# Attention by pairs of heads: 64-row score products side by side and a stacked position product

## The chip, the cores and the metric

The kernel runs on one core of a Trainium2 chip. The metric is the time of one execution on the device, in microseconds (us); the median of three runs before is 3395.38 us (3394.99 to 3407.65).

## What is computed

Two layers of a hybrid backbone over 1024 latent and 256 context tokens. Each layer mixes tokens by three parallel groups (latent attention with 8 heads, a convolution, a long convolution "hyena") and then runs an expert mixture. The change is in the attention:

```python
s = (jnp.einsum('bqhd,bkhd->bhqk', qn, k_nope, ...)      # 64 position-free dims
     + jnp.einsum('bqhr,bkr->bhqk', qr, k_rope, ...))    # 32 rotated dims, one key for all heads
w = jax.nn.softmax(s * scale, axis=-1).astype(v.dtype)
return jnp.einsum('bhqk,bkhd->bqhd', w, v)
```

Latent queries read 1280 keys (latent and context), context queries the 256 context keys (layer 0 only).

## The kernel before

Products that need more than one pass of precision are split: an operand `x` is kept as `xh` and `xl` (`hilo`, ScalarE rounds, VectorE subtracts), and `mm3` (lines 93 to 97) makes three products, high by high, high by low, low by high, into one bank of PSUM.

In `mla` the heads are taken one by one. For each head `K0`/`K1` (128 x 1280) holds 64 rows of position-free keys, the 32 rows of the rotated key, copied in by `fixed`, a row of ones and zeros; `Q0`/`Q1` (128 x 1024) holds the query the same way, with minus the greatest score of each query in row 96. So one product over 128 rows gives the score less its maximum. The maxima come from `largest`: a 96-row product of high parts for each 128 queries and up to 512 keys into a bank `p`, a VectorE reduction `mx`, and at the end a transposition `p<-ident,m` that puts the maxima into row 96.

`attend` runs units: a unit is one key tile of 128 keys and two lanes of 512 queries. For each lane `score` makes three products into a bank `s` (two banks), and ScalarE's exponential writes `pt`. `pv` makes the value product `o`: the two lanes go to columns 0 to 63 and 64 to 127 of the array. GpSimd adds up the `pt` for the denominators (`psum`). In a window of ten units (one head) the steps of `prepare` for the next head (`queries`, `keys`, `largest`) are dealt out over slots between the units. Before a window's last unit the rest of the steps is emitted at once. The convolution and `hyena` are emitted behind the first window and the scheduler moves them into gaps; what stands where on an engine is settled at build time, each engine then runs its list in order. `heads` loads the weights of the next head on SyncE's queue.

PSUM has eight banks: `s=2, o=1, p=3, hx=1, ha=1` (`hx` and `ha` are for the convolution and hyena).

Of the kernel before, what the change touches and what calls it, by code (L numbers as in the profile page):

```python
# [51 lines left out]
class Kernel:  # L52
# [17 lines left out]
    def banks(self, es, **tags):  # L70

        assert sum(tags.values()) <= 8
        self.n += 1
        pool = es.enter_context(self.tc.tile_pool(name=f"psum{self.n}", bufs=1, space=bass.MemoryType.PSUM, reuse_waits="tile"))

        def ps(tag, shape=(128, 512)):
            self.n += 1
            return pool.tile(list(shape), F32, name=f"{tag}{self.n}", tag=tag, bufs=tags[tag])
        return ps
# [317 lines left out]
    def win(self, l, M):  # L397
# [3 lines left out]
        with ExitStack() as es:  # L401
# [3 lines left out]
            with ExitStack() as es2:  # L405
# [24 lines left out]
                for g0, g1 in ((0, 4), (4, 8), (8, 10)):  # L430
# [65 lines left out]
                    S.activation(M["kr"][64:96, sl], tq[3][0:32, :N], AF.Copy)  # L496
                    V.tensor_tensor(M["kr"][96:128, sl], tq[3][0:32, :N], M["kr"][64:96, sl].bitcast(F32), ALU.subtract)
            with ExitStack() as es2:
# [3 lines left out]
                self.heads(l, 0, M)  # L502
                sc = self.t(P, [128, 6, 4], F32, "scols", bufs=1)
# [91 lines left out]
    def mla(self, l, M):  # L595
# [3 lines left out]
        with ExitStack() as es:  # L599
            P = self.pool(es, f"mla{l}", 2, **({} if last else {"side": "right"}))  # L600
            H = self.pool(es, f"hy{l}", 1)
            ps = self.banks(es, s=2, o=1, p=3, hx=1, ha=1)
# [4 lines left out]
            Qs, Ks, Cs = [], [], []  # L607
            for i in range(2):
                Qs.append(operand(f"Q{i}", 1024))
                Ks.append(operand(f"K{i}", 1280))  # L610
                Cs.append(None if last else operand(f"QC{i}", 256))

            def fixed(i):

                K = Ks[i]
                S.activation(K[0][64:96, :], M["kr"][64:96, :].bitcast(F32), AF.Copy)
                S.activation(K[1][64:96, :], M["kr"][96:128, :].bitcast(F32), AF.Copy)
                G.memset(K[0][96:128, :].bitcast(F32), 1.0)
                G.memset(K[1][96:128, :].bitcast(F32), 0.0)
                for Q in (Qs[i], Cs[i]):  # L620
                    for x in Q or ():
                        G.memset(x[96:128, :].bitcast(F32), 0.0)

            Vt = [None] * 10
            self.turned = {}

            def values(i):

                wr = self.t(P, [128, 512], F32, "rd", bufs=1)[:, :256]
                wh, wl = (self.t(M["pool"], [128, 2, 128], F32R, f"wq{x}", bufs=1).rearrange("p a b -> p (a b)") for x in "hl")  # L630
                nc.sync.dma_start(wr, A["w_v"][l][:, 256 * i:256 * i + 256])
                self.hilo(wh, wl, wr)
                for k in range(10):
                    p = ps("p")[:, :256]
# [6 lines left out]
            def prepare(h):  # L641

                K, Q, QC = Ks[h % 2], Qs[h % 2], Cs[h % 2]
                if h == 0:
                    fixed(0)
                elif h == 1:
                    with self.tc.issue_after(self.turned[0].ins):
                        fixed(1)
                yield from self.queries(P, ps, l, h, M, Q, QC, tab)
                yield from self.keys(P, ps, l, h, M, K)  # L650
                yield from self.largest(P, ps, K, Q, 1024, 0, 1280, h == 0)
                if QC:
                    yield from self.largest(P, ps, K, QC, 256, 1024, 256, h == 0)

            windows = []
            for h in range(8):
                w = []
                if h % 2 and not last:
                    w += self.attend(P, ps, l, [(h - 1 + j, Ks[j], Cs[j], 0, 256, 1024) for j in range(2)], Vt, range(8, 10))
                w += self.attend(P, ps, l, [(h, Ks[h % 2], Qs[h % 2], c, 512, c) for c in (0, 512)], Vt, range(10))  # L660
                windows.append(w)
            units = [u for w in windows for u in w]
            vals = values(0)
            for i, _ in enumerate(prepare(0)):
                if i >= 6:
                    next(vals, None)
            for _ in vals:
                pass
            units[0].score(0)
            units[0].score(1)  # L670
            n, later = 0, []
            for h, w in enumerate(windows):

                chain, steps = (prepare(h + 1), 33 if last else 38) if h < 7 else (iter(()), 0)
                vals, valued = values(1) if h == 3 else None, 0
                taken, slots = 0, 3 * len(w) - SLACK[l]
# [6 lines left out]
                for i, u in enumerate(w):  # L683
                    if n + 1 < len(units):
# [3 lines left out]
                        units[n + 1].score(0)  # L688
                        slot(3 * i)
                        units[n + 1].score(1)  # L690
                    slot(3 * i + 1)
# [6 lines left out]
                    slot(3 * i + 2)  # L698
# [10 lines left out]
    def queries(self, P, ps, l, h, M, Q, QC, tab):  # L709

        nc, A, S, V, G = self.nc, self.A, self.S, self.V, self.G
        wr = M["wq"]
        wh = self.t(M["pool"], [128, 2, 128], F32R, "wqh", bufs=1)
        wl = self.t(M["pool"], [128, 2, 128], F32R, "wql", bufs=1)
        self.hilo(wh, wl, wr)
        kr, kh, kl = M["wk"], self.t(M["pool"], [128, 64], F32R, "wkh", bufs=1), self.t(M["pool"], [128, 64], F32R, "wkl", bufs=1)
        self.hilo(kh, kl, kr)
        M["wkhl"] = kh, kl
        if h < 7:
            with self.tc.issue_after(self.loaded.ins):  # L720
                self.heads(l, h + 1, M)
        for c, N in ((0, 512), (512, 512), (1024, 256))[: 3 if QC else 2]:
            p = ps("p")
            s = slice(c, c + N)
# [23 lines left out]
    def largest(self, P, ps, K, Q, nq, k0, nk, first):  # L748

        V = self.V  # L750
# [84 lines left out]
    def hyena(self, l, M, P, ps):  # L835
# [12 lines left out]
        def table(src):  # L848

            t = self.t(P, [128, 2, 512], F32R, "ht", bufs=6)[:, :, :src.shape[2] * src.shape[3]].rearrange("p h (k m) -> p h k m", k=src.shape[2])  # L850
            with self.tc.issue_after(self.turned[0].ins):
                G.dma_start(t, src)
# [947 lines left out]
```

## Time and profile before

| | |
|---|---|
| median of three runs | 3395.38 us |
| the profiled execution | 3398.4 us, its span 3396.6 us |
| PE (TensorE), DVE (VectorE), ACT (ScalarE), POOL (GpSimd) busy | 3126.6, 2532.4, 1691.3, 1300.8 us |
| attention stage of layer 0 | about 500 to 975 us |
| attention stage of layer 1 | about 2200 to 2625 us |

Matmuls are pipelined on PE, and an instruction's duration holds a tail that lies beside the next one; what a product costs in a stream is the distance from its start to the next start. The name behind an arrow is written from the names after it, so `s<-Q1h,K1h` is a score with moving queries and stationary keys. `128*64` is rows by columns of the array in use.

### The profile page before, as it was taken

How to read it: one execution, taken by the hardware profiler on the slowest of the kernel's cores; microseconds unless marked ns; L12 is line 12 of the kernel's file. 1: busy time of each engine (PE TensorE's matmuls, PEld its weight loads, DVE VectorE, ACT ScalarE, POOL GpSimd, SP SyncE). 2: the span in 40 equal slices, each digit the busy share in tenths (PEclk: the TensorE clock that was granted, in tenths of full speed). 3: DMA queues.
4: the chain of work that ended last, by engine and by line, in shares of the span. 5: the costliest groups of instructions: out<-in, count | busy, mean ns of one | idle time of the engine just before them, and what ended most of it. 6: DMA issues, size and time to landing. Idle time of an engine off the chain costs nothing. (4 is left out here: it accounts for less than half of the span.)

```text
span 3396.6 us, 42699 instructions
## 1 busy us (share of the span) xinstructions
PE 3126.6 (92%) x15595; PEld 2226.8 (66%) x15595; DVE 2532.4 (75%) x3507; ACT 1691.3 (50%) x2447; POOL 1300.8 (38%) x1130
## 2 busy tenths in 40 slices
PE   7898989999999699999999969899999959999996
PEld 2467865666567466666666657656664747888885
DVE  7755698777667677777777646977775769998986
ACT  4315235433443356555665543353435427777775
POOL 4431255754654312211211112565557423433334
PEclk9898989999999799999999979899999979999998
DMA  8981112231253477777777621221223459999994
GB/s 304 324 272 60 38 64 82 54 101 45 73 162 116 179 288 280 275 298 279 289 280 284 217 95 44 82 70 51 69 93 115 151 225 356 385 378 372 380 379 173
DMA packets 138075, 660.80 MB, mean 195 GB/s; under 512 B 20520, under 2 KB 58824, under 8 KB 107145
## 3 DMA queue, kind: packets, MB, share of 16 engines
q1 hardware_dynamic: 112681, 582.85, 45.7%
q0 software_dynamic: 24768, 74.05, 7.9%
q8 instruction: 123, 2.02, 0.2%
q10 hardware_dynamic: 416, 1.18, 0.1%
q14 instruction: 87, 0.71, 0.1%
HBM read 589.24 MB, written 68.78 MB: 194 GB/s over the span
## 5 line engine op out<-in xcount | busy, mean ns | idle before, releaser
L91 DVE TENSOR_TENSOR mwl<-raw,mwh 128x1024 fp32r<-128x1024 f32 x710 | 883.4, 1281 | 215.8 <-ACT mwh L90 203.6
L90 ACT ACTIVATE mwh<-raw 128x1024 fp32r<-128x1024 f32 x768 | 791.0, 1057 | 347.9 <-PE acc L97 112.3
L96 PE MATMUL acc<-mwl,xh 128*128 128x512 f32 x1024 | 404.3, 395 | 0.5 <-DVE idc L1371 0.5
L97 PE MATMUL acc<-mwh,xl 128*128 128x512 f32 x1024 | 401.7, 394 | 0.1
L95 PE MATMUL acc<-mwh,xh 128*128 128x512 f32 x1024 | 371.4, 400 | 6.3 <-ACT xh L90 5.9
L803 POOL TENSOR_TENSOR psum<-psum,pt 128x512 f32<-128x512 f32 x252 | 333.1, 1341 | 68.3 <-ACT pt L788 64.4
L788 ACT ACTIVATE pt<-s 128x512 f32<-128x512 f32 (+1 forms) x336 | 196.0, 587 | 251.9 <-PE s L97 209.7
L1500 POOL DMA_INDIRECT xd<-ymoe,idx x31 | 105.5, 3404 | 544.5 <-DVE ymoe L1496 468.0
L758 DVE TENSOR_REDUCE mx<-p 128x1 f32<-128x512 f32 (+1 forms) x374 | 204.2, 584 | 65.0 <-PE p L100 64.2
L95 PEld LDWEIGHTS acc<-mwh,xh 128*128 128x128 f32 x1024 | 191.4, 189 | 69.0 <-ACT mwh L90 11.3
L96 PEld LDWEIGHTS acc<-mwl,xh 128*128 128x128 f32 x1024 | 192.9, 188 | 43.8 <-DVE mwl L91 2.5
L91 POOL TENSOR_TENSOR mwl<-raw,mwh 128x1024 fp32r<-128x1024 f32 x58 | 150.0, 2591 | 183.2 <-ACT mwh L90 121.1
L97 PEld LDWEIGHTS acc<-mwh,xl 128*128 128x128 f32 x1024 | 191.8, 188 | 39.5 <-issue 0.8
L100 PE MATMUL o<-pt,Vt 128*64 128x512 f32 (+1 forms) x672 | 184.1, 611 | 0.0
L564 DVE SCALAR_TENSOR_TENSOR cacc<-pad,cw,cacc 128x1295 f32<-128x1295 f32 (+1 forms) x90 | 165.7, 1842 | 1.3
L97 PE MATMUL mm<-hTh,wfl 128*128 128x512 f32 (+1 forms) x400 | 151.4, 380 | 12.8 <-DVE wfl L91 12.8
L95 PE MATMUL mm<-hTh,wfh 128*128 128x512 f32 (+1 forms) x400 | 152.7, 382 | 4.0 <-ACT wfh L90 4.0
L96 PE MATMUL mm<-hTl,wfh 128*128 128x512 f32 (+1 forms) x400 | 152.1, 380 | 0.0
L562 POOL TENSOR_TENSOR cacc<-cacc,tap 128x1295 f32<-128x1295 f32 (+1 forms) x30 | 97.0, 3233 | 120.8 <-ACT tap L561 118.7
L100 PE MATMUL cx<-raw,xcT 128*32 128x512 f32 x1024 | 124.0, 597 | 0.0
L95 PE MATMUL mm<-woh,yhh 128*128 128x512 f32 x280 | 114.8, 413 | 6.7 <-ACT wt L1128 3.8
L96 PE MATMUL mm<-wol,yhh 128*128 128x512 f32 x280 | 112.1, 401 | 0.0
(539 smaller groups left out, 7245.3 us busy)
## 6 DMA issues: line engine op xcount, KB each, us to landing
raw<-in_w_gate_dram SPq DMA_DIRECT2D x64, 2048.0 KB
raw<-in_w_up_dram SPq DMA_DIRECT2D x64, 2048.0 KB
raw<-in_w_down_dram SPq DMA_DIRECT2D x64, 2048.0 KB
mw<-in_mod_w_dram SPq DMA_DIRECT2D x48, 1024.0 KB
ht<-in_k_C_dram POOLq DMA_DIRECT2D x24, 512.0 KB, 5.1
wfr<-in_w_fm_dram SPq DMA_DIRECT2D x20, 512.0 KB
hd<-h SPq DMA_DIRECT2D x18, 512.0 KB
fw<-in_k_filt_dram POOLq DMA_DIRECT2D x17, 512.0 KB, 5.2
```

Of the source, the lines that this page charges most:

```text
L90: self.S.activation(hi, src, AF.Copy)
L91: (eng or self.V).tensor_tensor(lo, src, hi.bitcast(F32), ALU.subtract)
L95: mm(out, ah, bh, start=first, stop=False, skip_group_check=True)
L96: mm(out, ah, bl, start=False, stop=False, skip_group_check=True)
L97: return mm(out, al, bh, start=False, stop=last, skip_group_check=True)
L100: return self.T.matmul(out, a, b, start=first, stop=last, skip_group_check=True)
L562: G.tensor_tensor(a, a, t, ALU.add)
L564: V.scalar_tensor_tensor(a, x, w2[:, ct, k:k + 1], a, ALU.mult, ALU.add)
L758: V.tensor_reduce(mx[:, q, n:n + 1], p[:, :N], AX.X, ALU.max)
L788: S.activation(pt[:, :N], p[:, :N], AF.Exp, scale=ATT_SCALE)
L803: (V if tail and n > 8 else G).tensor_tensor(sm[:, :N], st.sums[i][:, :N], pt[:, :N], ALU.add)
L1500: G.indirect_dma_start(self.xd[l], bass.IndirectOffsetOnAxis(ap=d["idx"], axis=0), y, None, compute_op=ALU.add)
```

## The change

Heads are taken in pairs. The position-free part of the keys and queries of two heads is stacked, 64 rows each, in one operand (`K0h`/`K0l`, `Qh`/`Ql`), and each product on it is made as two, on rows 0 to 63 and 64 to 127, with results in two banks. The rotated part gets operands of its own: `ks` holds the rotated key of all heads as high, low, high rows and four rows of minus one; `Rh` and `Rl` (one for each head of the pair) hold the rotated query in the matching order and the maxima. One product over 128 rows with `ks` so gives the whole position part and subtracts the maximum.

- A unit is now one key tile, two heads and 512 queries: six 64-row products and two 128-row products, as before six products of 128 rows. A window is a pair of heads and a chunk of 512 queries.
- `largest` makes, for each 128 queries and key chunk, two 64-row products for the position-free part and two for the rotated part (rows 0 to 63 of `ks` with the first head's `Rh`, rows 64 to 127 with the second's), and one reduction over both banks. The maxima go back through two transpositions and two VectorE products with the identity.
- Keys of two heads come from one product of 128 columns.
- Banks: `ss=(1, 2), o=1, pp=(1, 2), p=1, hx=1, ha=1`: one pair for the scores, one pair for the maxima, and one bank `p` for everything else.
- Weights are loaded once per pair, results are written once per pair, hyena's `fe` and `hg` get other buffers.

```diff
-            ps = self.banks(es, s=2, o=1, p=3, hx=1, ha=1)
+            ps = self.banks(es, ss=(1, 2), o=1, pp=(1, 2), p=1, hx=1, ha=1)
...
-                chain, steps = (prepare(h + 1), 33 if last else 38) if h < 7 else (iter(()), 0)
+                g, c = (h + 1) // 2, (h + 1) % 2
+                chain, steps = (prepare(g, c), (16 if last else 20) if c else 19) if h < 7 else (iter(()), 0)
-                taken, slots = 0, 3 * len(w) - SLACK[l]
+                taken, slots = 0, 2 * len(w) - SLACK[l]
...
+    def queries(self, P, ps, l, M, Q, c, N, tab, first=False):
...
+        for j, (one, two, low) in enumerate(((0, 32, 64), (64, 32, 0))):
+            r, x = Q[1][j], tq[32 * j:32 * j + 32, :]
+            S.activation(r[one:one + 32, :], x, AF.Copy)
+            S.activation(r[two:two + 32, :], x, AF.Copy)
+            V.tensor_tensor(r[low:low + 32, :], x, r[one:one + 32, :].bitcast(F32), ALU.subtract)
...
-            self.mm3(p[0:64, :N], wh, wl, M["kvh"][:, s], M["kvl"][:, s], True, True)
-            self.hilo(K[0][0:64, s], K[1][0:64, s], p[0:64, :N])
+            self.mm3(p[:, :N], wh, wl, M["kvh"][:, s], M["kvl"][:, s], True, True)
+            self.hilo(K[0][:, s], K[1][:, s], p[:, :N])
...
-                p = ps("sspp"[q % 4] if first else "p")
-                self.mm(p[:, :N], Q[0][0:96, 128 * q:128 * q + 128], K[0][0:96, c:c + N])
-                V.tensor_reduce(mx[:, q, n:n + 1], p[:, :N], AX.X, ALU.max)
+                s = slice(128 * q, 128 * q + 128)
+                pp = ps("ss" if first and q % 2 else "pp")
+                for j in (0, 1):
+                    r = slice(64 * j, 64 * j + 64)
+                    self.mm(pp[j][:, :N], Qn[0][r, s], K[0][r, c:c + N], True, False)
+                for j in (0, 1):
+                    r = slice(64 * j, 64 * j + 64)
+                    self.mm(pp[j][:, :N], R[j][r, s], ks[r, c:c + N], False, True)
+                V.tensor_reduce(mx[:, :, q, n], pp[2][:, :, :N], AX.X, ALU.max)
...
-            def score(i):
-                _, K, Q, c, _, _ = lanes[i]
-                p = ps("s")
-                self.scored = self.mm3(p[:, :N], K[0][:, s], K[1][:, s], Q[0][:, c:c + N], Q[1][:, c:c + N], True, True)
-                pt = u.pts[i] = self.t(P, [128, 512], F32, "pt", bufs=6)
-                S.activation(pt[:, :N], p[:, :N], AF.Exp, scale=ATT_SCALE)
+            def score():
+                p = ps("ss")
+                with self.tc.high_priority(6000):
+
+                    for i, (a, b) in enumerate(((0, 0), (0, 1), (1, 0))):
+                        for j in (0, 1):
+                            r = slice(64 * j, 64 * j + 64)
+                            self.mm(p[j][:, :N], K[a][r, s], Qn[b][r, :N], i == 0, False)
+                    for j in range(2):
+                        self.scored = self.mm(p[j][:, :N], ks[:, s], R[j][:, :N], False, True)
+                for j in range(2):
+                    pt = u.pts[j] = self.t(P, [128, 512], F32, "pt", bufs=6)
+                    S.activation(pt[:, :N], p[j][:, :N], AF.Exp, scale=ATT_SCALE)
...
-                with self.tc.high_priority(400), self.tc.issue_after(self.scored.ins):
+                with self.tc.high_priority(6000), self.tc.issue_after(self.scored.ins):
```

Where the instructions stand. First PE in the last window of layer 1, one unit: `s` and `ss` are scores, `o` the value product, `Vt` the values. Before:

```order
L95 MATMUL s_21733<-Q1h_17874,K1h_17876 128x512
L96 MATMUL s_21733<-Q1l_17875,K1h_17876 128x512
L97 MATMUL s_21733<-Q1h_17874,K1l_17877 128x512
L95 MATMUL s_21739<-Q1h_17874,K1h_17876 128x512
L96 MATMUL s_21739<-Q1l_17875,K1h_17876 128x512
L97 MATMUL s_21739<-Q1h_17874,K1l_17877 128x512
L100 MATMUL o_21623<-pt_21721,Vt_4570_20601 64x512
L100 MATMUL o_21623<-pt_21727,Vt_4570_20601 64x512
```

Here six full products stand between two value products. After:

```order
L105 MATMUL ss_21504<-Q1h_17768,K1h_17762 128x512 x2
L105 MATMUL ss_21504<-Q1l_17769,K1h_17762 128x512 x2
L105 MATMUL ss_21504<-Q1h_17768,K1l_17763 128x512 x2
L105 MATMUL ss_21504<-R1h_17770,ks_16228 128x512
L105 MATMUL ss_21504<-R1l_17771,ks_16228 128x512
L105 MATMUL o_21389<-pt_21496,Vt_4180_20422 64x512
L105 MATMUL o_21389<-pt_21498,Vt_4180_20422 64x512
```

The three rows with x2 are the pairs on 64 rows, then come the two position products on 128 rows; the next unit begins with 64-row products again.

Second, PE at the end of the window before that one, where the last steps of `largest` stand. Before (`p<-K1h,Q1h` is a step of `largest`):

```order
L100 MATMUL p_21493<-K1h_17876,Q1h_17874 128x512
L95 MATMUL s_21571<-Q0h_17870,K0h_17872 128x512
L96 MATMUL s_21571<-Q0l_17871,K0h_17872 128x512
L97 MATMUL s_21571<-Q0h_17870,K0l_17873 128x512
L100 MATMUL p_21502<-K1h_17876,Q1h_17874 128x256
L95 MATMUL s_21583<-Q0h_17870,K0h_17872 128x512
L96 MATMUL s_21583<-Q0l_17871,K0h_17872 128x512
L97 MATMUL s_21583<-Q0h_17870,K0l_17873 128x512
L100 MATMUL o_21351<-pt_21544,Vt_4578_20635 64x512
L100 MATMUL o_21351<-pt_21553,Vt_4578_20635 64x512
```

A step of `largest` stands between scores, and those left over follow `o`. After:

```order
L105 MATMUL pp_21300<-K1h_17762,Q1h_17768 128x256 x2
L105 MATMUL pp_21300<-ks_16228,R1h_17770 128x256
L105 MATMUL pp_21300<-ks_16228,R1l_17771 128x256
L105 MATMUL pp_21310<-K1h_17762,Q1h_17768 128x256 x2
L105 MATMUL pp_21310<-ks_16228,R1h_17770 128x256
L105 MATMUL pp_21310<-ks_16228,R1l_17771 128x256
L794 MATMUL p_21335<-ident_60,m_4359_21329 4x128 x2
L105 MATMUL ss_21357<-R1h_17770,ks_16228 128x512
L105 MATMUL ss_21357<-R1l_17771,ks_16228 128x512
L105 MATMUL o_21109<-pt_21349,Vt_4193_20477 64x512
L105 MATMUL o_21109<-pt_21351,Vt_4193_20477 64x512
```

Steps of `largest` (each x2 and two single rows, all on 64 rows) now stand one behind the other on the one pair `pp`, then the transposition, then the two 128-row products of a score whose 64-row products stand ahead of these steps.

## Rows read from the trace of the kernel before

**Rows 1.** The page, part 1: engine, busy us, share, instructions.
```profile
PE 3126.6 (92%) x15595; PEld 2226.8 (66%) x15595; DVE 2532.4 (75%) x3507; ACT 1691.3 (50%) x2447; POOL 1300.8 (38%) x1130
```

**Rows 2.** Windows: stretch, length, busy (count) of PE, PEld, DVE, ACT, POOL; clock, DMA share, GB/s.
```profile
500.00:975.00 475.00, 448.79 (x2174) 286.11 (x2173) 345.43 (x598) 207.84 (x409) 280.81 (x283) 0.97 0.25 73
2200.00:2625.00 425.00, 401.75 (x1857) 251.91 (x1857) 301.34 (x485) 178.95 (x340) 262.38 (x252) 0.97 0.26 80
```

**Rows 3.** Timeline of PE, layer 1's last window: start, us, line, tiles, shape.
```profile
2603.20 0.50 PE L95 MATMUL s<-Q1h,K1h 128*128 128x512 f32 x1
...
2603.77 0.40 PE L97 MATMUL s<-Q1h,K1l 128*128 128x512 f32 x1
...
2604.23 0.40 PE L96 MATMUL s<-Q1l,K1h 128*128 128x512 f32 x1
2604.47 0.40 PE L97 MATMUL s<-Q1h,K1l 128*128 128x512 f32 x1
2604.79 1.08 PE L100 MATMUL o<-pt,Vt 128*64 128x512 f32 x4
2605.80 0.50 PE L95 MATMUL s<-Q1h,K1h 128*128 128x512 f32 x1
```

**Rows 4.** Timeline of PE in the filter stage, products on one row.
```profile
153.49 0.39 PE L100 MATMUL p<-exl,er 1*128 1x512 f32 x1
153.80 0.50 PE L95 MATMUL p<-dh,fw 128*128 128x512 f32 x1
...
164.67 0.40 PE L97 MATMUL p<-dh,fw 128*128 128x512 f32 x1
165.00 0.50 PE L100 MATMUL p<-exh,er 1*128 1x512 f32 x1
165.34 0.39 PE L100 MATMUL p<-exl,er 1*128 1x512 f32 x1
```

**Rows 5.** Timeline of PE in layer 0's experts, transposes on 64 rows.
```profile
1209.65 0.40 PE L96 MATMUL acc<-mwl,xh 128*128 128x512 f32 x1
1209.98 0.66 PE L1481 MATMUL dt<-ident,hc 64*64 64x64 f32 x8
1210.57 0.49 PE L97 MATMUL acc<-mwh,xl 128*128 128x512 f32 x1
```

**Rows 6.** Timeline of PE in layer 0's attention, products of 256 columns.
```profile
701.31 0.28 PE L97 MATMUL hx<-hT,ht 128*128 128x256 f32 x1
701.43 0.28 PE L95 MATMUL p<-qh,wqh 128*128 128x256 f32 x1
```

**Rows 7.** Timeline of PE in layer 0's attention, a key product.
```profile
707.62 0.39 PE L96 MATMUL s<-Q1l,K1h 128*128 128x512 f32 x1
707.85 0.39 PE L95 MATMUL p<-kvh,wkh 128*64 128x512 f32 x1
```

**Rows 8.** Groups by line and shape, 500 to 975 us: count, busy, mean ns.
```profile
L788 ACT ACTIVATE pt<-s 128x512 f32<-128x512 f32 x160 | 94.7, 597 | 122.0 <-PE s L97 88.5 <-PE o L100 17.9 <-POOL psum L803 12.4
L100 PE MATMUL o<-pt,Vt 128*64 128x512 f32 x320 | 89.4, 625 | 0.0
L758 DVE TENSOR_REDUCE mx<-p 128x1 f32<-128x512 f32 x120 | 77.6, 678 | 22.6 <-PE p L100 22.3
L758 DVE TENSOR_REDUCE mx<-p 128x1 f32<-128x256 f32 x74 | 27.6, 415 | 16.0 <-PE p L100 15.8
L817 DVE RECIPROCAL rd<-rd 128x512 f32<-128x512 f32 x8 | 26.8, 3345 | 2.0 <-ACT rd L816 1.9
```

**Rows 9.** Waits of PE, 500 to 975 us: total us, times, longest.
```profile
PE p L100 <- DVE mx L758: 1.0, 3, 0.5
```

**Rows 10.** Timeline of PE, transposes of the maxima in layer 1.
```profile
2584.40 1.03 PE L768 MATMUL p<-ident,m 128*1 128x128 f32 x8 [1.20 <-DVE m L762]
```

**Rows 11.** Timeline of ACT, layer 1's last window.
```profile
2604.26 1.29 ACT L788 ACTIVATE pt<-s 128x512 f32<-128x512 f32 x2 [1.31 <-PE s L97]
```

**Rows 12.** Timeline of POOL, layer 1's last window.
```profile
2601.20 8.94 POOL L803 TENSOR_TENSOR psum<-psum,pt 128x512 f32<-128x512 f32 x7
```

More of the change, by code (lines that the diff above doesn't have):

```diff
@@ L70, in banks @@
     def banks(self, es, **tags):
-        assert sum(tags.values()) <= 8
+        tags = {k: v if isinstance(v, tuple) else (v, 1) for k, v in tags.items()}
+        assert sum(a * b for a, b in tags.values()) <= 8
         self.n += 1
@@ L77, in ps @@
             self.n += 1
-            return pool.tile(list(shape), F32, name=f"{tag}{self.n}", tag=tag, bufs=tags[tag])
+            n, size = tags[tag]
+            if size == 1:
+                return pool.tile(list(shape), F32, name=f"{tag}{self.n}", tag=tag, bufs=n)
+            both = pool.tile([128, size, 512], F32, name=f"{tag}{self.n}", tag=tag, bufs=n)
+            return [both[:, j] for j in range(size)] + [both]
         return ps
@@ L639, in values @@
                     yield
[L641 to L653, printed above, removed]
@@ L655, in mla, with prepare @@
-            windows = []
[L656 to L661, printed above, removed]
+            def prepare(g, c):
+                K, Q = Ks[g % 2], Qs[c]
+                if g == 0:
+                    fixed(Q)
+                    if c and Cs:
+                        fixed(Cs)
+                first = g == c == 0
+                if c == 0:
+                    yield from self.weights(P, l, g, M)
+                elif g < 3:
+                    with self.tc.issue_after(self.loaded.ins):
+                        self.heads(l, g + 1, M)
+                yield from self.queries(P, ps, l, M, Q, 512 * c, 512, tab, first)
+                if first:
+                    self.turned = self.rotated
+                if c == 0:
+                    yield from self.keys(P, ps, l, M, K, first)
+                elif Cs:
+                    yield from self.queries(P, ps, l, M, Cs, 1024, 256, tab)
+                yield from self.largest(P, ps, M, K, Q, 512, 0, 1280, first)
+                if c and Cs:
+                    yield from self.largest(P, ps, M, K, Cs, 256, 1024, 256, False)
@@ L662, in mla @@
+            windows = []
+            for g in range(4):
+                for c in range(2):
+                    w = []
+                    if c and not last:
+                        w += self.attend(P, ps, l, M, g, Ks[g % 2], Cs, 1024, 256, Vt, range(8, 10))
+                    windows.append(w + self.attend(P, ps, l, M, g, Ks[g % 2], Qs[c], 512 * c, 512, Vt, range(10)))
             units = [u for w in windows for u in w]
             vals = values(0)
-            for i, _ in enumerate(prepare(0)):
-                if i >= 6:
+            for i, _ in enumerate(prepare(0, 0)):
+                if i >= 7:
@@ L687, in mla @@
                                 pass
[L688 to L691, printed above, removed]
+                        units[n + 1].score()
+                    slot(2 * i)
                     u.pv()
@@ L763, in largest @@
+        self.negated = V.tensor_reduce(m1[:, :, :qt], mx[:, :, :qt, :len(kch)], AX.X, ALU.max)
         yield
[L764 to L772 removed]
+        p = ps("p")
@@ L774, in attend @@
         nc, S, V, G = self.nc, self.S, self.V, self.G
-        N = lanes[0][4]
-        tail = lanes[0][0] == lanes[1][0] == 7
+        tail = g == 3 and at == 512
+        ks, (Qn, R) = M["ks"], Q
         st = SimpleNamespace(o=None, sums=[None, None])
```

161 lines of the change are left out of this document (76 added, 85 removed).

## Prediction

> **What bounds the kernel now.** I read the page first. TensorE (PE) is busy 92% of the span, the other engines 38 to 75% [rows 1]. The change touches the two attention stages, so I took the windows 500 to 975 us (layer 0) and 2200 to 2625 us (layer 1): PE is busy 448.8 of 475 us and 401.8 of 425 us there, VectorE (DVE) 345 and 301, ScalarE (ACT) 208 and 179, GpSimd (POOL) 281 and 262, at a granted clock of 0.97 [rows 2]. Both stages are bound by PE's instruction stream, so the change is worth what it takes from or adds to that stream; PE's own idle time is only about 25 us a stage.
>
> The timeline of PE gives prices start to start. A product with 512 columns follows another after 0.23 us (2604.23 to 2604.47) [rows 3], one with 256 columns after 0.12 us [rows 6]. One unit (two lanes, one key tile) in layer 1's last window is six score products and the value product `o`: 2603.20 to 2605.80, 2.60 us [rows 3]. Around `o` there are gaps no dependency explains: the last score product before it starts at 2604.47 and `o` at 2604.79, 0.10 us more than the pitch; the first product after it (2603.20) carries 0.50 us where the others carry 0.39 to 0.40, 0.11 us more. `o` is the only product there that uses half of the array's columns twice, side by side.
>
> The same signature stands where few rows are used. Products on one row: 164.67 to 165.00 (0.10 late), then 165.34 (0.11 late) [rows 4]; back to full rows, 153.49 to 153.80 (0.08 late), with 0.50 us on the product [rows 4]. The transposes of `hc`, on 64 rows: 1209.65 to 1209.98, 0.10 late, and the product behind them again carries 0.49 us [rows 5]. So a change between full and split array costs **0.21 us** (0.10 + 0.11). One case is free: the key products `p<-kvh,wkh`, 64 columns wide but alone, stand among full ones at the plain pitch (707.62 to 707.85) [rows 7].
>
> **The change, part by part.**
>
> *Score products.* Before: six full slots a unit. After: six 64-row products in two halves of the array, plus two full position products. If the halves run side by side, that is 3 + 2 = 5 slots. Side by side is shown for columns: 320 records of `o` at 0.625 us would be 200 us and take 89.4 [rows 8]; rows are not shown. I take it as full. 160 units x 0.228 + 8 context units x 0.12 = **-37.4 us**.
>
> *Keys.* One 128-column product serves two heads: per head three groups of three, 3 x (0.228 + 0.228 + 0.117) = 1.72 us; eight heads become four pairs in each of two layers: 8 x 1.72 = **-13.7 us**. Queries (2 x 6 products a chunk) and values stay. *Transposes* of the maxima: 144 become 40; eight span 1.03 us, about 0.9 without the last one's tail [rows 10], 0.11 each: **-11.4 us**.
>
> *Maxima.* A step was one 96-row product; now it is a pair of 64-row products and a pair for the position part, for two heads: the same slots if pairs overlap. DVE's reduction is twice as wide and half as often: 0.678 us for 512 and 0.415 for 256 elements [rows 8] give 1.03 ns an element over 0.15, so 1.21 us for 1024 where two took 1.36. DVE gets no busier.
>
> *Changes of the array's split.* Every unit now has one inside its score (64-row to full rows), and every maximum step that lies between full products has two. The pieces of the order shown ahead of this prediction have both kinds; counted over the whole order as changes between full array, 64-row halves and side-by-side columns, there are 193 and 173 in the two layers before and 421 and 370 after. (The free cases above, and the transposes, are not counted.) +425 x 0.21 = **+89 us**. Bounds: 0, by the keys [rows 7], and 0.21. I take 0.21, because the 64-row transposes and the one-row products are rows, as the new ones are.
>
> A rule of the Trainium skill speaks against the change here: "TensorEngine Tiling (Array Packing)", section Tiling Modes, says that a change of the tiling mode, not of the tile, drains the engine; by it each of the 425 costs a drain, as in the sum. The key products speak against it as a general rule; by them alone the term would be 0. The same page's overview promises up to 2x for 64 rows, which is the -37.4 above and no more.
>
> *Buffers.* Maxima had three banks, and now one pair (`pp`). PE waits for the reduction whenever two steps follow each other with nothing between. In the order that happens 36 times, at window ends: 11 after a 512-column step, 25 after a 256-column one. The bare reductions are 11 x 1.21 + 25 x 0.68 = **+30 us**. Before, PE waited only 1.0 us for `mx` in layer 0 [rows 9]. Bounds: 0 (if other waits stood there anyway) and 66 (also the steps with too little between, by the same count).
>
> The scores also get one pair of banks (`ss`) instead of two that alternate. Both exponentials wait for the last of the eight products, and the next score waits for both. An exponential starts 0.49 us after the start of its last product (2603.77 to 2604.26 [rows 3, 11]) and a pair back to back takes 2 x 0.597 [rows 8]. With 0.06 for the signal back, an estimate, the next score starts about 1.75 us after the last product, while PE has only the 0.33 to `o` and `o`'s 1.01 to do: 0.42 us short. 24 units have only `o` between: **+10 us**. Such a unit would take 2.57 by PE alone (five slots, three changes, `o`) and 2.99 with the wait, against 2.60. POOL, with two sums of 1.28 us (8.94 / 7) in such a unit [rows 12], stays under that.
>
> *At nothing:* the copies into `ks`, the memsets, and half as many weight loads of twice the size lie in stages where SyncE and ACT have room (ACT under half busy [rows 2]); the shared `gt` buffers can delay hyena's gate loads, which the second half of each stage covers. Without cover that is 5 or 6 us. The rotation moves some ACT and DVE work about, within a few us.
>
> *Sum:* -37.4 - 13.7 - 11.4 + 89 + 30 + 10 = **+66.5 us**. The profiled execution took 3398.4 us (span 3396.6), 3.0 over the median of 3395.4; against the median, 3395.4 + 66.5 = **3462 us**.
>
> **Rivals.**
>
> *Changing the split costs nothing* for these products, as for the keys [rows 7]. Then 89 goes and 3395.4 - 22.5 = 3373 us, **faster**. It decides at 22.5 / 425 = 0.05 us a change: below that the change wins. Against it: three kinds of rows at 0.2 [rows 3 to 5]. At half price the result is 3418 us.
>
> *The halves don't run side by side.* Then the score's 64-row products are 240 slots more a layer, the maxima 128 of 512 and 64 of 256 columns, plus the context: 2 x 91.6 + 5 = 188 us, so 3650 us. For it: no row shows two row halves at once; against it: column halves do overlap [rows 8].
>
> *The one pair `pp` ties PE to DVE's backlog.* A reduction stands behind whatever DVE does, above all the reciprocals, eight a layer of 3.35 us [rows 8]. With three banks PE ran on; with one it stops. 16 x 3.35 = 54 us on top: 3516 us. For it: DVE is busy 71 to 73% in the stages [rows 2]; against it: there is other work for PE in most units.
>
> **How the numbers follow.** Forecast 3462 us, own range 3420 to 3510, chance 0.58. Free changes, 3373: 0.12. Half price or the like, within 0.5% (17 us, about what a measurement can tell): 0.10. DVE's backlog, 3516: 0.12. Serial halves, 3650: 0.08. The range 3373 to 3535 leaves out the serial case and about half of the fastest. Faster 0.12, same 0.10, slower 0.78.
>
> **What would show it.** In the profile after: score pairs of 64-row products at 0.23 us a pair, not a product; the first position product of each unit with 0.50 us and a start 0.10 late; units of the last window at about 3.0 us, with PE waiting for ACT `pt`; PE waiting some 15 us a layer for DVE `mx`; stages about 25 to 40 us longer. If the position products follow the pairs at the plain pitch, the largest term is wrong and the kernel is about even or faster.

## The result and the profile after

The changed kernel takes 3582.09 us (3578.43 to 3588.61), the kernel before beside it 3400.79: a ratio of 1.0534 with the interval 1.0504 to 1.0564, **181 us slower**. The forecast was 66.5 us slower, and its range ended at 3535. The direction was right, the size was not.

The profiled execution has a span of 3579.8 us. From the last product of the input projection to the first of the output projection, layer 0's attention takes 556.3 us (497.9 to 1054.2) where it took 476.8, layer 1's 518.3 (2277.4 to 2795.7) where it took 442.1: 156 of the 183 us between the two spans. The other 27 lie outside: 6 before layer 0's attention, 13 between it and the first expert, 8 behind layer 1's attention. Part 1 of the page answers to [rows 1], the two windows to [rows 2] (length, busy and count of PE, PEld, DVE, ACT, POOL, then clock):

```profile
PE 3203.7 (89%) x16155; PEld 2199.1 (61%) x16155; DVE 2500.5 (70%) x3269; ACT 1677.0 (47%) x2429; POOL 1265.5 (35%) x1126
```

```profile
497.90:1054.20 556.30, 481.20 (x2451) 268.00 (x2449) 332.99 (x478) 199.78 (x401) 268.02 (x284) 0.90 0.18 56
2277.40:2795.70 518.30, 442.90 (x2173) 239.16 (x2171) 300.35 (x404) 179.77 (x349) 258.21 (x262) 0.90 0.20 66
```

The kernel before, in the same bounds:

```profile
491.60:968.50 476.90, 447.41 (x2164) 284.70 (x2162) 349.29 (x605) 210.44 (x412) 284.23 (x286) 0.96 0.25 73
2179.00:2621.00 442.00, 413.15 (x1902) 260.24 (x1901) 319.11 (x515) 189.30 (x356) 271.38 (x261) 0.96 0.25 79
```

PE is idle for 75 us in each stage, where it was 29, and the granted clock has fallen from 0.96 to 0.90. By the trace's record of the clock PE stands at the lower of its two levels (1.2 instead of 2.4 GHz) for 107 + 108 us of the two stages; before it was 34 + 35.

A unit with work behind it, on PE's timeline in layer 0 (start, us, line, tiles, shape), answers to [rows 3]:

```profile
942.49 0.39 PE L105 MATMUL ss<-Q1h,K0h 64*128 64x512 f32 x2
942.72 0.39 PE L105 MATMUL ss<-Q1l,K0h 64*128 64x512 f32 x2
942.95 0.40 PE L105 MATMUL ss<-Q1h,K0l 64*128 64x512 f32 x2
943.27 0.50 PE L105 MATMUL ss<-R1h,ks 128*128 128x512 f32 x1
943.62 0.39 PE L105 MATMUL ss<-R1l,ks 128*128 128x512 f32 x1
943.94 1.08 PE L105 MATMUL o<-pt,Vt 128*64 128x512 f32 x4
944.95 0.50 PE L105 MATMUL pp<-K1h,Q0h 64*128 64x512 f32 x2
945.28 0.39 PE L105 MATMUL pp<-ks,R0h 64*128 64x512 f32 x1
945.29 0.39 PE L105 MATMUL pp<-ks,R0l 64*128 64x512 f32 x1
945.51 0.39 PE L105 MATMUL ss<-Q1h,K0h 64*128 64x512 f32 x2
```

Two 64-row products start together and the next two 0.23 us later (942.49, 942.72, 942.95): the halves do run side by side. The first position product comes 0.09 late with 0.50 us, and its follower another 0.11 late (943.27 to 943.62): 0.20 for the change of the split, as forecast. No wait stands in this unit. The waits stand at the end of a window:

```profile
952.30 0.39 PE L105 MATMUL pp<-K1h,Q0h 64*128 64x256 f32 x2
...
953.59 0.39 PE L105 MATMUL pp<-K1h,Q0h 64*128 64x256 f32 x2 [0.79 <-DVE mx L787]
...
954.88 0.38 PE L105 MATMUL pp<-K1h,Q0h 64*128 64x256 f32 x2 [0.79 <-DVE mx L787]
...
956.38 0.38 PE L794 MATMUL p<-ident,m 128*4 128x128 f32 x2 [1.00 <-DVE m L790]
957.54 0.80 PE L105 MATMUL ss<-R0h,ks 128*128 128x512 f32 x1 [0.77 <-DVE R0h L796]
958.13 0.80 PE L105 MATMUL ss<-R0l,ks 128*128 128x512 f32 x1
958.86 1.98 PE L105 MATMUL o<-pt,Vt 128*64 128x512 f32 x4
```

Steps on the one pair `pp` follow each other every 1.29 us (952.30, 953.59, 954.88), where their two pairs of 256 columns would take 0.24 at the 0.12 us of [rows 6]; then the chain maxima, transposition, rows of R is waited out in full. The products that follow run at half rate (0.80 instead of 0.40, `o` 1.98 instead of 1.08): PE has stood still for 3.35 of the last 4.7 us, and the clock is at its lower level. PE's waits in the two stages (total us, times, longest), first layer 0, then layer 1, against [rows 9]:

```profile
PE pp L105 <- DVE mx L787: 30.7, 29, 4.1
PE p L794 <- DVE m L790: 7.6, 5, 2.0
...
PE ss L105 <- ACT pt L824: 3.4, 15, 0.3
```

```profile
PE pp L105 <- DVE mx L787: 32.2, 30, 3.5
PE p L794 <- DVE m L790: 5.7, 4, 2.7
...
PE ss L105 <- ACT pt L824: 4.8, 15, 1.0
```

### The profile page after: what moved, and what is told of

The parts are those of the page before. It is cut to its first block, busy times and chain, and to the rows that moved or that the text cites. A ratio compares the mean times of both kernels' runs of the same rounds, so it can differ in the third digit from the quotient of the medians.

```text
span 3579.8 us, 43381 instructions
## 1 busy us (share of the span) xinstructions
PE 3203.7 (89%) x16155; PEld 2199.1 (61%) x16155; DVE 2500.5 (70%) x3269; ACT 1677.0 (47%) x2429; POOL 1265.5 (35%) x1126
## 5 line engine op out<-in xcount | busy, mean ns | idle before, releaser
L824 ACT ACTIVATE pt<-ss 128x512 f32<-128x512 f32 (+1 forms) x336 | 179.8, 585 | 344.1 <-PE ss L105 336.7
L787 DVE TENSOR_REDUCE mx<-pp 128x2 f32<-128x1024 f32 (+1 forms) x188 | 193.3, 1028 | 99.4 <-PE pp L105 98.4
```

The source lines that it names most:

```text
L787: V.tensor_reduce(mx[:, :, q, n], pp[2][:, :, :N], AX.X, ALU.max)
L824: S.activation(pt[:, :N], p[j][:, :N], AF.Exp, scale=ATT_SCALE)
```

## The experiments

Times are medians; "changed" is the changed kernel at 3582 us. My theory after the trace: the one pair `pp` holds PE at the windows' ends, and the lower clock behind it doubles the loss. Its rivals: the chain behind the maxima holds the windows' ends whatever the banks; the changes of the split cost more than they show; they cost nothing.

**A faster reduction.**

```diff
-                V.tensor_reduce(mx[:, :, q, n], pp[2][:, :, :N], AX.X, ALU.max)
+                V.tensor_reduce(mx[:, :, q, n], pp[2][:, :, :32], AX.X, ALU.max)
```

> The changed kernel, but each reduction of the maxima reads 32 instead of up to 512 keys of each bank (64 elements for 1024 or 512), so that DVE frees the pair pp after about 0.2 us instead of 1.23 or 0.69; the maxima are then wrong, and the exponential takes a 64th of its scale so that nothing overflows. Products and their order stay nearly as they are. Theory (the waits for pp, and the lower clock behind them, are what the sum missed): PE's 63 us of waiting for DVE mx in the two stages fall under 15, the time at the lower clock in the stages (now 108 + 112 us) falls by a quarter or more, and the kernel gains 50 to 85 us: 3495 to 3530. Rival A (window ends are held by the chain behind the maxima, the transposition and the rows written back, and a faster reduction only moves the wait there): 20 us or less, 3560 or more. Rival B (changes of the split cost more than 0.21 us and make up the rest): 10 us or less.

Measured: 3508.4 us, 74 less. PE's waits of `pp` for `mx` went from 63 to 26 us (37 times, the longest 5.5) and the time at the lower clock in the stages from 215 to 125. Both rivals fall; but more of the wait is left than the theory's 15 us.

**A second pair where hyena has left its banks.**

```diff
+                two = (not first) and spare and q % 2
+                pp = [ps("hx"), ps("ha")] if two else ps("ss" if first and q % 2 else "pp")
...
+                    for j in (0, 1):
+                        V.tensor_reduce(mx[:, j, q, n:n + 1], pp[j][:, :N], AX.X, ALU.max)
```

> The changed kernel, but from the sixth window on, where hyena is done with its two banks, every second step of the maxima goes to those two banks, each reduced by itself (two reductions of about 0.68 us instead of one of 1.23). So PE has a second pair to write while DVE reduces the first. Theory (one pair is the cause of the waits): of the 36 us that PE waits for DVE mx after 860 us in layer 0 and after 2595 us in layer 1 at least 25 go, and with them some 10 to 20 us of lower clock: 3535 to 3550. Rival (DVE's own rate or the chain to the transposition holds the window's end, whatever the buffers): the wait moves to the transposition, 10 us or less, above 3570.

Measured: 3524.9 us, 57 less, more than expected. The end of layer 1's attention in both kernels, after hyena, with the same work (first the changed kernel, then this one):

```profile
2595.40:2782.00 186.60, 154.16 (x701) 66.11 (x701) 79.82 (x82) 59.18 (x108) 95.28 (x75) 0.88 0.14 54
```

```profile
2568.80:2727.30 158.50, 144.46 (x703) 64.32 (x701) 80.72 (x100) 59.28 (x109) 95.33 (x76) 0.97 0.17 64
```

28 us less in 187: PE is idle for 14.0 us instead of 32.4, and the same products are busy for 9.7 us less, at a clock of 0.97 instead of 0.88. DVE was not the limit: it does more reductions in less time. Windows after hyena take 39.5 and 39.6 us instead of 48.7 and 48.0 (from one copy of `o` to the next); before the change the one such window took 39.4.

**The banks of before, throughout.** This was run among the last, to see whether the pair accounts for all that the sum lacks.

```diff
-            ps = self.banks(es, ss=(1, 2), o=1, pp=(1, 2), p=1, hx=1, ha=1)
+            ps = self.banks(es, ss=(1, 2), o=1, p=3, hx=1, ha=1)
...
-                pp = ps("ss" if first and q % 2 else "pp")
+                both = first and q % 2
+                pp = ps("ss") if both else [ps("p"), ps("p")]
```

> The changed kernel with the banks for the maxima as before: no pair pp, but three single banks p for the maxima and everything else; a step of the maxima takes two of them, one for each head, and each is reduced by itself (two reductions of 0.68 us instead of one of 1.23). Theory (the single pair costs the time that the sum lacks): the windows without hyena come down from 48 us to about 40 as in e4_pp2, and those with hyena too; 14 windows x 8 to 9 us, so 110 to 130 us less than the changed kernel: 3450 to 3475, near the forecast of 3462. Rival (the second pair helped only where hyena's banks were free, because there it did not share p with queries, keys and values): 3520 or more.

Measured: 3471.6 us, **110 less**, at a ratio of 1.0198 (1.0181 to 1.0215) to before: 65 us slower than the kernel before beside it, 71 slower than the one beside the changed kernel; the forecast was 66.5. Both versions have three banks for the maxima and everything else. What this run undoes is that two of them are taken, reduced and released as one and serve the maxima alone; which of these it is was not taken apart. The two stages:

```profile
495.70:1003.90 508.20, 468.31 (x2451) 268.72 (x2449) 339.73 (x575) 197.59 (x400) 272.76 (x284) 0.95 0.20 60
2227.60:2688.80 461.20, 428.84 (x2172) 241.70 (x2172) 306.09 (x494) 178.50 (x349) 259.27 (x262) 0.96 0.23 74
```

They are 105 us shorter than in the changed kernel (969.4 and 1074.6). PE's idle time is 78 us of that (72 instead of 150); the other 27 is that the same products (4623 and 4624) are busy for 897.2 instead of 924.1 us. The same place, the end of a window in layer 1:

```profile
2644.59 0.39 PE L105 MATMUL p<-K1h,Q1h 64*128 64x256 f32 x2
...
2645.83 0.28 PE L105 MATMUL p<-ks,R1l 64*128 64x256 f32 x1
2646.84 0.38 PE L799 MATMUL p<-ident,m 128*4 128x128 f32 x2 [0.73 <-DVE m L795]
2647.15 1.08 PE L105 MATMUL p<-psum,ones 128*64 128x512 f32 x4
2648.16 0.50 PE L105 MATMUL ss<-R1h,ks 128*128 128x512 f32 x1
2648.59 0.50 PE L105 MATMUL ss<-R1l,ks 128*128 128x512 f32 x1
```

Steps follow each other without a wait, one short wait is left, and the products behind it run at full rate. PE's waits for `mx` are 2.2 us in layer 0 and not among the longest seven in layer 1; the time at the lower clock is 55 + 37 us.

**The same coupling put into the kernel before.**

```diff
-            ps = self.banks(es, s=2, o=1, p=3, hx=1, ha=1)
+            ps = self.banks(es, s=2, o=1, p=2, pm=1, hx=1, ha=1)
...
-                p = ps("sspp"[q % 4] if first else "p")
+                p = ps(("s", "s", "p", "p")[q % 4] if first else "pm")
```

> The kernel before with one thing of the change alone: the maxima get one bank (pm) of their own instead of sharing three (p=2, pm=1), everything else as it was, whole heads, products on full rows. Counted over the order, two steps of the maxima now follow each other with nothing between 171 times in all, 91 after a step on 512 keys and 80 after one on 256. Theory (a single place for the maxima makes PE wait for the reduction, and the clock follows): 91 x 0.678 + 80 x 0.415 = 95 us of waits, with the lower clock behind them 100 to 140 us more: 3505 to 3545. Rival (the changed kernel's waits come from its wider reductions or its order, not from the single place): within 15 us of before, 3390 to 3420.

Measured: 3653.2 us, 248 more than before: the theory, but twice its price. PE's timeline in layer 1 and its waits in the two layers:

```profile
2756.01 0.50 PE L100 MATMUL pm<-K0h,Q0h 96*128 96x512 f32 x1 [0.79 <-DVE mx L758]
2757.30 0.49 PE L100 MATMUL pm<-K0h,Q0h 96*128 96x512 f32 x1 [0.78 <-DVE mx L758]
```

```profile
PE pm L100 <- DVE mx L758: 58.3, 84, 3.4
```

```profile
PE pm L100 <- DVE mx L758: 63.9, 87, 3.9
```

The two stages, against those of the kernel before:

```profile
490.30:1089.90 599.60, 504.25 (x2163) 303.68 (x2162) 352.37 (x605) 211.71 (x412) 282.68 (x286) 0.86 0.19 58
2303.90:2874.30 570.40, 470.83 (x1902) 279.66 (x1901) 313.60 (x515) 190.18 (x356) 266.27 (x261) 0.85 0.20 62
```

A step that takes 0.23 us in a stream takes 1.29, so it loses 1.06, not the 0.68 of the reduction. The waits list only 0.79 of that; the other 0.27 is the product's tail, which now has nothing beside it. The listed waits are 122 us in 171 steps; with 0.27 for each, 46 us, they come to 168 of the 248. The time at the lower clock rises by 272 (from 69 to 341), and 80 us are left for it. The windows say much the same: the same products (4066 and 4065) are busy for 975.1 instead of 860.6 us, and 114 less 46 is 68. So the clock took some 70 to 80 us, 0.25 to 0.29 for each microsecond at the lower level. This split is worked out, not measured; that the clock doubles the loss, as the theory had it, is not borne out.

**Without maxima**, in both kernels: products, reductions, transpositions and written rows are left out.

> The kernel before without the maxima: their products, reductions, transpositions and the rows written back are left out (nothing is subtracted from the scores, and the exponential takes a 64th of its scale); queries, keys, scores, values and sums stay. It is the base for the next run. By the slots alone: 240 steps of 0.23 us, 134 of 0.12 and 144 transposes of 0.11 us are 87 us, so about 3318 us.

> The changed kernel without the maxima, in the same way. What is left of the change is the scores (37.4 us less), the keys (13.7 less), the pair ss (10 more) and the changes of the split: counted over the order 352 + 305 here against 210 + 190 in the run before without maxima, 257 more, at 0.21 us 54 more. Theory (the sum is right but for the maxima, and the one pair pp is what cost the rest): 13 us more than the run before without maxima, and up to 40 more with the 27 us that were found outside the attention. Rival (the changes of the split or the pair ss cost far more than counted, and the maxima only carry part of the loss): 80 us more or beyond. Second rival (changes are free in the total, as the run with paired position products would have it): 40 us less, to 15 less with what was found outside.

Measured: 3332.9 and 3311.4 us. The changed kernel is now 21.5 us faster, so maxima cost it 271 us, and the kernel before 74 (3407.4 beside it). By the numbers as they stand this is the second rival, not the theory. But the base is disturbed: without maxima the kernel before ends its attention with hyena alone, and PE then stands still (layer 0):

```profile
925.01 1.02 PE L100 MATMUL st<-ones,ysq 128*128 128x1 f32 x4 [20.78 <-POOL ysq L1080]
```

Such waits and those for `woh` behind them are 56 us in its two layers, some 50 more than in the kernel before itself. Taken off, the changed kernel would be about 29 us slower, in the theory's 13 to 40; that is worked out, not measured, and the comparison of the two alone doesn't decide between theory and second rival.

**What a change of the split costs in the total.** Full rows, in scores and maxima:

```diff
-                        for j in (0, 1):
-                            r = slice(64 * j, 64 * j + 64)
-                            self.mm(p[j][:, :N], K[a][r, s], Qn[b][r, :N], i == 0, False)
+                        self.mm(p[0][:, :N], K[a][:, s], Qn[b][:, :N], i == 0, False)
```

> The changed kernel with every pair of 64-row products replaced by one product on all 128 rows, in the scores and in the maxima: the same number of slots if pairs run side by side, but no change between 64-row halves and full rows. The second head's position-free part is left out (scores and maxima are not the reference's; the exponential takes a 64th of its scale). Counted over the order, the changes of the split fall from 421 + 370 to 183 + 165, by 443. Theory (0.21 us a change, pairs fully side by side): 443 x 0.21 = 93 us less, 3489, with PE's waits for DVE mx left. Rival A (changes are free and the time went into waits alone): 3575 to 3590. Rival B (pairs overlap only in part): more than 93 us less, below 3470.

Measured: 3507.1 us, 75 less, 0.17 us a change: between the theory and rival A, and rival B falls. The same edit in the scores without maxima:

> The changed kernel without the maxima (as e12_nomax_after), and with every pair of 64-row products of a score replaced by one product on all 128 rows (the second head's position-free part is left out as well): the same slots, but 187 + 167 changes of the split instead of 352 + 305, 303 fewer, and no wait for the maxima that could take the gain back. Theory (0.21 us a change, in the total too): 64 us less than e12_nomax_after, 3240 to 3255. Half price: 32 us less, 3280. Rival (a change costs nothing in the total, as e3_pairs would have it): within 8 us of e12_nomax_after, 3303 to 3320.

Measured: 3268.2 us against 3311.4: 43 less, 0.14 us a change: not free, and nearer to half price (32 us) than to 0.21 (64).

Paired position products:

```diff
-                    for j in range(2):
-                        self.scored = self.mm(p[j][:, :N], ks[:, s], R[j][:, :N], False, True)
+                    for i, x in enumerate((ks, M["kt"])):
+                        for j in (0, 1):
+                            r = slice(64 * j, 64 * j + 64)
+                            self.scored = self.mm(p[j][:, :N], x[r, s], R[i][r, :N], False, i == 1)
```

> The changed kernel with the position product of a score also made as pairs of 64-row products: the rows of R are dealt out anew (first tile: the upper half for head one, the lower half for head two; second tile: the other halves) and a copy of ks with its halves exchanged is kept, so each head stays on its own 64 rows and its own bank. The slots stay at 5 a unit; a unit goes from three changes of the split to two. Counted over the order: 357 + 309 instead of 421 + 370, 125 fewer. Hyena's tables get five buffers instead of six to make room. Theory: 125 x 0.21 = 26 us less, 3556. Rival (changes cost nothing): no gain, 3582, or a few us more for the copies and the missing buffer.

Measured: 3583.6 us, nothing gained, though each unit did get shorter: from 3.02 us (942.49 to 945.51 above) to 2.84, on PE's timeline:

```profile
942.42 0.41 PE L105 MATMUL ss<-Q1h,K0h 64*128 64x512 f32 x2
...
943.12 0.41 PE L105 MATMUL ss<-R1h,ks 64*128 64x512 f32 x2
943.34 0.41 PE L105 MATMUL ss<-R1l,kt 64*128 64x512 f32 x2
...
945.26 0.41 PE L105 MATMUL ss<-Q1h,K0h 64*128 64x512 f32 x2
```

I blamed the missing table buffer first:

> The changed kernel with five buffers for hyena's tables instead of six and nothing else: the part of the run with paired position products (e3_pairs) that was only there to make room. Theory (changes of the split cost 0.2 us each, and the missing buffer ate the gain of that run): 15 to 30 us slower than the changed kernel, 3597 to 3612. Rival (the buffer doesn't matter, and the paired position products gained nothing by themselves): 3577 to 3587.

Measured: 3567.4 us, 15 *less*: that explanation falls. The planner makes the order anew for every edit; that the new order is what these 15 us are is likely, but not shown. Without maxima, with the same buffers on both sides:

> The changed kernel without the maxima and with paired position products (as e3_pairs, five table buffers): 259 + 224 changes of the split against 347 + 305 in the next run, 169 fewer. Theory: 169 x 0.21 = 35 us less than the next run, less about 5 for the two copies at the start of each attention: 25 to 35 less. Rival (no gain, as with the maxima): within 8 us of it.

> The changed kernel without the maxima and with five buffers for hyena's tables: the base for the run before. As with the maxima (e6_ht5 was 15 us faster than the changed kernel): 3295 to 3312. If that was only the order that the planner happened to make: anywhere within 15 us of e12_nomax_after.

Measured: 3302.6 and 3322.0 us, 19.4 less for 169 changes (0.11 us each, 0.14 if the copies cost 5), less than the theory's 25 to 35, and the missing buffer now costs 11 us. With single banks for the maxima:

> The same three single banks, with paired position products (five table buffers): 358 + 321 changes of the split against 422 + 388, 131 fewer. By the 0.14 us a change that e13 and e14 showed in the total 18 us less than e16_p3, within 10 either way; 3430 to 3455. Rival (the windows' ends take it back as in e3_pairs): the same as e16_p3.

Measured: 3468.4 us, 3 less than e16_p3: the rival. Its last window in layer 1, where no maxima are made, takes 25.4 us instead of 27.0, the two before it 38.3 and 36.5 instead of 39.0 and 36.4. So the gain is there in a window without maxima, and in these two windows with them it is mostly lost; that the waits for the maxima take it back fits this, and was not shown by itself.

**Three smaller ones.** `ks` at the end of its pool:

```diff
-                M = {"pool": MP, "ks": self.t(MP, [128, 1280], F32R, "ks"),
+                M = {"pool": MP, "tab": self.t(MP, [128, 1024], F32, "tab"),
...
-                     "tab": self.t(MP, [128, 1024], F32, "tab")}
+                     "ks": self.t(MP, [128, 1280], F32R, "ks")}
```

> The changed kernel with two persistent tiles exchanged in memory: ks moves from the front of its pool to the end, where tab was. In the changed kernel the first load of the output projection (rows_same, on SyncE's queue) is put into the memory of ks, which every score reads to the end of the attention; the profile shows SyncE waiting 21.4 us for the last ss there, with the loads of w_o behind it. Theory (this is the 12 us that the output projection of layer 0, and some 8 us that the rest of layer 1, take more than before): the loads of w_o are issued before the last unit, PE's waits of 8.8 us for woh and wol in layer 0 go, and the kernel gains 10 to 20 us: 3562 to 3572. Rival (the results of the last window, not the weights, hold the first product): 3 us or less.

Measured: 3580.7 us, no difference. In SyncE's queue the loads of `w_o` did move ahead, from 1046.33 to 1028.63 us. But PE still waits 5.6 us for `woh` and 3.5 for `wol`: ACT's copy of the weights stands in its list behind that of the results (`yhh`, which waits for the last `yin`). Why the planner put it there and not amid the attention, as before, I didn't settle.

All three together:

> Paired position products, the second pair of banks for the maxima after hyena, and ks at the end of its pool, together (with five table buffers). If the three are independent: 57 us less for the second pair as in e4_pp2, 10 to 20 for ks, and 26 for 125 fewer changes less what the missing buffer costs: 3485 to 3515. If the paired position products bring nothing of themselves: 3510 to 3520.

Measured: 3535.2 us, 10 more than e4_pp2 alone and above both expectations: the parts don't add up.

Filling the waits with products that nobody reads:

> The changed kernel with more work: in the last three windows of each layer, before the later steps of the maxima on 256 keys, three products of 512 columns into hyena's idle bank (0.69 us, 20 times, 14 us in all), whose result nobody reads. They stand where PE waits for DVE mx. Theory (PE's standing still at the windows' ends is what brings the clock down): PE's wait there falls, the time at the lower clock in the two stages falls from 215 us by 20 or more, and the kernel does not get slower in spite of 60 more products: 3565 to 3585. Rival (the lower clock has nothing to do with these waits): the time at the lower clock stays, and the kernel takes up to 14 us more, 3585 to 3596.

Measured: 3593.3 us, 11 more. The waits for `mx` after hyena fell from 36 to 22 us, the time at the lower clock by 10 only: the filled waits were not the last ones, the chain from the maxima to R's rows still stood open, and the products behind it still ran at half rate. So the theory missed both of its numbers (20 us less at the lower clock, and no slower), and the time is the rival's: filling some of a gap bought little of the clock back here and cost 11 of the 14 us put in.

One thing of the change alone, in the kernel before: a single transposition of the maxima.

```diff
-            for q in range(c // 128, (c + N) // 128):
-                self.T.transpose(p[0:1, 128 * q - c:128 * q - c + 128], m1[:, q:q + 1], self.ident)
-            self.S.activation(Q[0][96:97, c:c + N], p[0:1, :N], AF.Copy)
+        self.T.transpose(p[0:qt, 0:128], m1[:, :qt], self.ident)
```

> The kernel before with the other thing of the change that needs no pairs: the maxima of a head are turned by one transposition of 8 columns instead of eight of one, and DVE spreads them with the identity over eight rows (keys hold minus one there) instead of ACT copying one row. Transposes fall from 144 to 20; at 0.11 us each that is 124 x 0.11 = 14 us if they stand on PE's path, against two DVE products of 0.68 us a head. Theory: 5 to 15 us faster than before, 3390 to 3400. Rival (PE waits there for the maxima anyway, and the transposes were cover): within 5 us of before.

Measured: a ratio of 1.001 (0.9996 to 1.0024): no difference, the rival. (The edit also puts two DVE products in the place of ACT's copies, which could hide a gain of a few us.) No version that does all the work beats the kernel before.

## Why the prediction was wrong, step by step

- **Scores, -37.4: right** in mechanism; pairs at 0.23 us, five slots a unit. The serial rival's 3650 is 68 us from the result, about as near as the backlog rival's 3516 (66) and nearer than the forecast (120), and yet it is refuted by the timeline; a near number is no proof. **Keys, -13.7**: not tried alone.
- **Transposes, -11.4: wrong.** 124 fewer in the kernel before gave nothing: PE waits there for the maxima anyway ([rows 10] has the 1.20 us in its brackets), so they probably had cover.
- **Changes of the split, +89: right at each place, too large in the total.** 0.20 to 0.21 in the stream; in the total 0.14 to 0.17 by e2_full and e13_nomax_full, 60 to 72 us, but 0.11 by e14_nomax_pairs and next to nothing in e3_pairs and e17_p3pairs. The rival "free" falls, since 43 and 75 us are more than the 11 and 15 us that the edit of one table buffer moved; "half price" (0.105) does not fall. The rule of the Trainium skill that was weighed ("TensorEngine Tiling (Array Packing)", Tiling Modes: a new mode drains the engine) agrees with the timeline, where such a change costs 0.20 us; it states no price.
- **The one pair `pp`, +30: the step that failed; it cost 110** (e16_p3). Three things were wrong in it. It counted the 36 steps that follow one another with nothing between, though its own bound of 66 had the others: PE waited 59 times, 63 us. It took the bare reduction for the loss, where the cycle of product, reduction and signal counts: a step every 1.29 us where 0.24 would do, so 1.05 lost against the 0.68 in the sum. And it had no price for the clock: the stages spent 146 us more at the lower level than before. But its part is bounded: e16_p3 takes 122 us at the lower level away, and the same products are then busy for 27 us less, tails included, so in PE's busy time the clock is at most a quarter of the 110. Whether steps dealt out with other work between them would have avoided the waits on the same pair was not tried.
- **The backlog rival, 3516,** had the right place and the wrong reason. Its reductions were to wait behind reciprocals; but 40 of the 59 waits stand after hyena, none over 1.3 us: before 37 of the 40 reductions DVE was idle, for 0.60 us or more, and it simply took its time. A true backlog is seen a few times in the first windows (the 4.1 us above).
- **The single pair `ss`, +10: right**: 30 waits, 8.2 us. A unit of the last window takes 2.86 us, where 2.99 was expected:

```profile
1039.85 0.50 PE L105 MATMUL ss<-Q1h,K1h 64*128 64x512 f32 x2 [0.23 <-ACT pt L824]
...
1042.71 0.50 PE L105 MATMUL ss<-Q1h,K1h 64*128 64x512 f32 x2 [0.23 <-ACT pt L824]
```

- **"At nothing": wrong by 27 us** outside the attention; some 12 us of it are the output projection of layer 0, where PE waits 8.8 us for weights that now get ready only after the last window. The 27 are not the pair's: with e16_p3 21 of them stay. The wait for memory was not the cause (e5_ks); the rest is open.

Put together: 110 for the pair in place of 30 is 80 more, the outside 21 more (6 of its 27 are in the 110), the transposes 11 more, the changes 17 to 29 less: 66.5 + 80 + 21 + 11 - 23 = 156 of the 181 us. With the smaller prices of a change the sum comes out lower still. The rest, 25 us or more, stays open; a new order alone may be worth some of it (15 us in e6_ht5). That e16_p3 lands on the forecast is partly luck: its stages are only 50 us longer than before and 21 lie outside, which the forecast had at nothing, so its errors partly cancel.

## What to carry to other kernels

When an edit takes buffers away, price the full cycle of the ring (write, read, signal), for every step that has less than that cycle of other work in front of it, and test the price first by starving the old kernel of the same buffers, which is a two-line edit (it gives the direction; here its 248 us were more than twice the 110). A wait on PE is worth more than its listed length: the product before it loses its overlap (0.27 us here), and some of those behind it can run at the lower clock. And a slot that is removed in front of a wait can come back as wait: look at the chain that ends the window before the products in it.

## What was not expected of the hardware

- The lower clock cost far less than the time spent at it: in e9_one 272 us more at 1.2 GHz went with 70 to 80 of the 248 us; in the end of layer 1's attention 701 products were busy for 154.2 us at a clock of 0.88, and 703 for 144.5 at 0.97.
- Two products of 64 rows each take the place of one in the stream (0.23 us a pair), with no loss that these rows show.
- A change of the split of 0.20 us on the timeline was worth 0.11 to 0.17 us in the total in three comparisons and next to nothing in two: PE's time and the kernel's time are not the same even where PE is busy 90%.
